# Six of 22 half-pairs of a feed-forward block's second product, by seven quarter products in place of eight

## The chip, the cores and the metric

The kernel runs on one core of a Trainium2 chip. The metric is the device time of one execution in microseconds (us). Five engines of the core work side by side, each through its own queue in order: PE (TensorE, the matrix products; PEld is its weight load), DVE (VectorE), ACT (ScalarE), POOL (GpSimd) and SP (SyncE, which issues the loads). They wait for each other by semaphores. SBUF holds the data in 128 partitions; products land in PSUM, eight banks of 128 x 512 float32 numbers.

## The reference, cut to what matters

One decoder layer on 512 tokens of width 1024, in float32. It is a sandwich: a feed-forward block, a token mixer (two kinds of recurrent heads), and a second feed-forward block, each with a norm ahead and one behind. The change concerns both feed-forward blocks.

```python
def swiglu_ffn(x, w_in, w_out):                       # w_in 1024 x 5632, w_out 2816 x 1024
    gate, up = jnp.split(x @ w_in, 2, axis=-1)
    return (jax.nn.silu(gate) * up) @ w_out           # "second product": 512 x 2816 by 2816 x 1024

x = x + 0.5 * rms_norm(swiglu_ffn(rms_norm(x, norm_pre[l, 0]), ffn1_w_in[l], ffn1_w_out[l]), norm_post[l, 0])
x = x +       rms_norm(token_mixer(rms_norm(x, norm_pre[l, 1]), ...), norm_post[l, 1])
x = x + 0.5 * rms_norm(swiglu_ffn(rms_norm(x, norm_pre[l, 2]), ffn2_w_in[l], ffn2_w_out[l]), norm_post[l, 2])
```

## The kernel before, in words

**Three matmuls for one product.** PE multiplies in the type float32r. To keep float32 accuracy each operand is split into a high part (a copy by ACT, which rounds) and a low part (a subtraction by DVE), and `mm3` (L125) issues three matmuls: high by high, high by low, low by high (L127, L128, L129). An operand so split is called a tile here; making one is a *cast*, one ACT copy and one DVE subtraction over 128 x 1024 numbers. A matmul keeps a 128 x 128 block (the stationary side, PEld) in the array and moves 256 or 512 columns through it.

**First product** (`ffn_in`, L654, and `prod`, L476). It already goes by a seven-product scheme (p1 to p7, in an order written down in `ORDER`), with matmuls of 256 columns at L489. Its results, after SiLU and the product with the up half, are kept in `hf` (22 x 512 numbers in each partition: the hidden activations, transposed).

**Second product** (`ffn_out`, L676). The 2816 hidden rows are cut in 11 *pairs* of 256 rows, and the 1024 outputs in two halves of 512 columns. A pair in one half is a *half-pair*: 256 rows by 512 tokens by 512 columns, 24 matmuls of 512 columns (four blocks of 128 tokens, two blocks of rows, three matmuls each, L690). The loop at L701 goes over the 11 pairs, half 0 first, into four PSUM banks `acc`, one for each block of 128 tokens. For each half-pair it needs one weight tile and one activation tile:

- `pull` (L243) gives the next weight tile; `feed` and `split` (L186 to L226) cast weights ahead, in the order of a list of items (`ffn_items`), until WBUF = 4 tiles are alive or ready. Their four slots lie next to each other in one tensor `w`; `drop` (L250) frees a slot when its matmuls are done.
- `h_tile` (L666, casts L672 and L673) makes the activation tile in a ring of three buffers, two or three ahead (`more`).

After the first half-pair, the last of the seven products of the first product (p4 of the last tile) is done in between (L489, 24 matmuls). When half 0 is done, `post0` (L377) takes its squares (ACT L354) and its product with the gain (DVE L383). In half 1 the last four half-pairs (LAST = 4) are done block by block by `last` (L406): for each block `i` of 128 tokens the 24 matmuls that are left (six for each of the four pairs), then `post1` (L386: squares, two small POOL instructions L355 and L359, DVE L391 and L395), then `after(i)`: in the first block the next norm (`pre`, L362, DVE L373), in the second the store of the output. `trans` turns the normed tokens for the mixer (PE L268, ACT L274, DVE L275), and `head4` / `head_mm` (L439 to L455) starts the mixer's first four weight columns, 24 matmuls of 256 columns each (L444). `last` and what follows are put in order by the framework's scheduler; the order on each engine is then fixed in the program.

**Alignment.** `place` (L232), PAD, LATE and the `late` choice in `split` shift tiles by 64 to 448 bytes against each other.

Of the kernel before, what the change touches and what calls it, by code (L numbers as in the profile page):

```python
# [20 lines left out]
NF = FF // P  # L21
EPS = 1e-6
RAW, WBUF, PAD, LATE, NEAR = 3, 4, 128, 112, 48
PAIRS = NF // 2
HALF = T // 2
# [25 lines left out]
class Load:  # L51


    def __init__(self, key, src, a, b, ring="raw", depth=3, ahead=3, group=None):
        self.key, self.src, self.a, self.b, self.ring, self.depth, self.ahead = key, src, a, b, ring, depth, ahead
        self.group = group


class Item:

    def __init__(self, key, loads, rows=None, adds=(), dst=None):
        self.key, self.loads, self.rows, self.adds, self.dst = key, loads, rows, adds, dst
        self.reads = {key, *(k for pair in adds for k in pair)}


class Layer:
    def __init__(self, ctx, tc, aps):
        self.tc, self.nc = tc, tc.nc  # L70
        self.__dict__.update(aps)
        nc = self.nc
        pool = lambda name, **kw: ctx.enter_context(tc.tile_pool(name=name, bufs=1, **kw))
        self.cp, self.wp, self.sp, self.psp = pool("cp"), pool("wp"), pool("sp"), pool("psp", space=PSUM)
        self.dp = pool("dp", space=bass.MemoryType.DRAM)
        self.uid, self.hold = 0, ()
# [18 lines left out]
    def col(self, n=1):  # L95
        return self.sp.tile([P, n], F32, tag=f"col{n}", bufs={1: 12}.get(n, 4), name=self.name("col"))
# [89 lines left out]
    def split(self):  # L186

        nc = self.nc
        it = self.items.popleft()
        raw = self.raw[it.key]  # L190
        _, a, b = raw.shape
        if it.dst:
            w = it.dst()
        else:
            if self.wt is None:
                self.wt = self.wp.tile([P, 2 * D * WBUF + PAD], F32R, name="w")
# [7 lines left out]
            self.slot[id(w)] = n, late, w  # L204
        hi, lo = self.both(w)
        self.ready.append((w, it.dst is not None))
        rows = it.rows
        if rows is None:
            nc.scalar.copy(hi, raw)  # L209
            yield  # L210
            nc.vector.tensor_tensor(lo, raw, hi.bitcast(F32), op=ALU.subtract)  # L211
        else:
            for j in range(a):
                nc.scalar.activation(hi[:, j], raw[:, j], AF.Copy, scale=rows[:, j : j + 1])
            yield
            for j in range(a):
                nc.vector.scalar_tensor_tensor(
                    lo[:, j], raw[:, j], rows[:, j : j + 1], hi[:, j].bitcast(F32), op0=ALU.mult, op1=ALU.subtract
                )
        with self.behind(*self.hold):  # L220
            for out, other in it.adds:
                o, c = self.raw[out], self.raw[other]
                nc.gpsimd.tensor_tensor(o, o, c, op=ALU.add)  # L223
        self.load_due(self.done)
        self.done += 1
        yield  # L226

    def both(self, w):

# [41 lines left out]
    def two(self, dst, i, src):  # L271

        v = slice((i % 2) * P, (i % 2 + 1) * P)
        self.nc.scalar.copy(dst[:, 0, :, v], src)  # L274
        self.nc.vector.tensor_tensor(dst[:, 1, :, v], src, dst[:, 0, :, v].bitcast(F32), op=ALU.subtract)  # L275
# [387 lines left out]
        self.feed()  # L663
        self.lag()

    def h_tile(self, k2, dst=None):  # L666

        t = dst
        if t is None:
            t = self.place(self.hpool.tile([P, 2 * D + PAD], F32R, tag="s", bufs=3, name=self.name("hs")), 2)  # L670
        src = self.hf[:, 2 * k2 : 2 * k2 + 2, :]
        self.nc.scalar.copy(t[:, 0], src)  # L672
        self.nc.vector.tensor_tensor(t[:, 1], src, t[:, 0].bitcast(F32), op=ALU.subtract)  # L673
        return t

    def ffn_out(self, gpost_row, scale, after, trans, head):  # L676
        NK2, LAST = PAIRS, 4
        seq = [k2 for _ in range(2) for k2 in range(NK2)]
        hs = self.hs
        made = [len(hs)]  # L680

        def more(n):
            while made[0] < min(n, len(seq)):
                k2 = seq[made[0]]
                last = made[0] == len(seq) - 1
                dst = self.xq[3].rearrange("p b k t -> p b (k t)").rearrange("p b (k t) -> p b k t", k=2) if last else None
                hs.append(self.h_tile(k2, dst))
                made[0] += 1

        def out_mm(ps, w, h, k2, i):  # L690
            for kk in range(2):
                k = 2 * k2 + kk
                s = slice(i * P, (i + 1) * P)
                self.mm3(ps, h[:, 0, kk, s], h[:, 1, kk, s], w[:, 0, kk, :], w[:, 1, kk, :], k == 0, k == NF - 1)

        g = self.gain("gpost", gpost_row)
        ys = []
        n = 0
        for half in range(2):
            acc = [self.ps() for _ in range(NT)]  # L700
            for k2 in range(NK2 - LAST if half else NK2):  # L701
                more(n + 2)
                w = self.pull()
                more(n + 3)
                h = hs.popleft()
                for i in range(NT):
                    out_mm(acc[i], w, h, k2, i)
                self.drop(w)
                n += 1
                if n == 1:  # L710
                    self.prod("p4", PAIRS - 1)
                    self.after("p4", PAIRS - 1)
                self.lag()
            if half == 0:
                ys = [self.post0(acc[i], g, scale) for i in range(NT)]
        ws = []
        for k2 in range(NK2 - LAST, NK2):
            ws.append((k2, self.pull()))
            more(n + 1)
            n += 1  # L720
# [84 lines left out]
    def ffn_items(self, name, w_in, w_out):  # L805

        made = []
        place = {"p1": "a", "p2": "c", "p3": "d", "p4": "a", "p5": "a", "p6": "a", "p7": "b"}
        place.update({"c1": "a", "c2": "c", "c3": "b", "c4": "d"})
        adds = {}  # L810
# [21 lines left out]
        for p, t in ORDER:  # L832
            if p[0] == "e":
                continue
            dst = (lambda n=stay[p]: self.stay[n]) if p in stay else None
            made.append(Item((name, t, place[p]), own.get((p, t), ()), None, adds.get((p, t), ()), dst))
        for h in range(2):
            for k2 in range(PAIRS):
                src = w_out[k2 * 2 * P : (k2 + 1) * 2 * P, h * 512 : (h + 1) * 512].rearrange("(k p) d -> p k d", p=P)
                key = (name, "out", h, k2)  # L840
                made.append(Item(key, [Load(key, src, 2, 512, "raw2", 5, 8)]))
                if h == k2 == 0:
                    made.append(Item((name, PAIRS - 1, "a"), ()))
        return made

    def small_params(self):

# [711 lines left out]
```

## Time and profile before

| what | value |
|---|---|
| median of 3 runs | 937.39 us (937.3 to 937.43) |
| the profiled execution | 936.74 us, of which its span is 935.0 us |
| granted TensorE clock in it | 0.998 of full |
| PE busy / DVE busy / ACT busy / POOL busy | 926.7 / 700.1 / 468.7 / 289.9 us |
| matmuls | 7021 |
| first block: second product | about 225 to 350 us |
| second block: second product | about 806 to 928 us |

How to read it: the span is the time from the first to the last instruction of the profiled execution; a few microseconds of the execution lie around it. A busy engine is one that has an instruction in flight; neighbouring matmuls overlap, so the number that counts for PE is the distance from one start to the next. Rows of the groups give line, engine, operation, what is written and read, count, busy time and the mean of one in ns, and then the idle time ahead of them with the engine that ended it. In the table by stages each engine has its busy time and, in brackets, how many of its instructions touch the stretch; then come the granted clock (PEclk), the DMA share and GB/s.

### The profile page before, as it was taken

To read this page: it belongs to the slowest core of one execution; us is meant where nothing else is said; L and a number is where in the kernel's file an instruction comes from. 1 tells how busy PE (TensorE), PEld (TensorE's weight loads), DVE (VectorE), ACT (ScalarE), POOL (GpSimd) and SP (SyncE) were. 2 spreads that over 40 slices of the span, in tenths; PEclk is the share of its full clock that TensorE was granted. 3 is DMA by queue.
4 is the path that set the end of the run, shared out by engine and by line. 5 is a ranking of instruction groups with operands and counts; after the bars stand their busy time and mean duration, and the time that the engine had idled before them with its cause. 6 is when DMAs were issued, how large, how long until landed. Compare 5 with 4: busy or idle time off the path is not lost.

```text
span 935.0 us, 16820 instructions
## 1 busy us (share of the span) xinstructions
PE 926.7 (99%) x7021; PEld 850.6 (91%) x7021; DVE 700.1 (75%) x785; ACT 468.7 (50%) x639; POOL 289.9 (31%) x225
## 2 busy tenths in 40 slices
PE   9999999999999999999999999999999999999997
PEld 7999999999888889998888888999999999988885
DVE  6798999998545466688766655887999999844543
ACT  7645445455334345987654254853444454534431
POOL 3535555661000027000020301445455655100001
PEclk9999999999999999999999999999999999999999
DMA  9243334425323005422423135213333422332202
GB/s 318 89 136 114 113 97 131 128 99 158 113 91 106 7 3 126 108 83 70 136 70 113 46 108 185 90 46 113 114 111 117 134 91 91 116 110 91 91 0 91
DMA packets 81992, 97.10 MB, mean 104 GB/s; under 512 B 4178, under 2 KB 61558, under 8 KB 81915
## 3 DMA queue, kind: packets, MB, share of 16 engines
q1 hardware_dynamic: 81306, 94.44, 32.4%
q8 instruction: 55, 0.90, 0.4%
q0 software_dynamic: 320, 1.06, 0.3%
q10 hardware_dynamic: 288, 0.52, 0.2%
q14 instruction: 23, 0.18, 0.1%
HBM read 93.90 MB, written 2.11 MB: 103 GB/s over the span
## 4 chain that ended last, share of the span: by engine, by line
PE 97%; DVE 1%; POOL 1%; issue 1%; ACT 1%; DVEq 0%; POOLq 0%; ACTq 0%
PE ps L489 46%; PE ps L127 13%; PE ps L129 13%; PE ps L128 13%; PE ps L434 6%; PE ps L268 1%; PE ps L1058 1%; POOL col L355 0%; PE ps L1328 0%; PE ps L1131 0%; PE ps L1296 0%; PE ps L116 0%; ACT junk L354 0%; PE ps L123 0%; PE ps L1097 0%
## 5 line engine op out<-in xcount | busy, mean ns | idle before, releaser
L211 DVE TENSOR_TENSOR w<-raw,w 128x1024 fp32r<-128x1024 f32 x214 | 364.2, 1710 | 129.5 <-ACT w L209 129.5
L209 ACT CAST w<-raw 128x1024 fp32r<-128x1024 f32 x214 | 223.9, 1052 | 305.6 <-PE ps L129 104.5
L223 POOL TENSOR_TENSOR raw<-raw,raw 128x1024 f32<-128x1024 f32 x80 | 221.0, 2763 | 171.8 <-DVE w L211 161.3
L489 PE MATMUL ps<-xq,w 128*128 128x256 f32 x2016 | 238.1, 277 | 0.0
L489 PEld LDWEIGHTS ps<-xq,w 128*128 128x128 f32 x2016 | 233.7, 188 | 0.2
L489 PE MATMUL ps<-sq,w 128*128 128x256 f32 x1440 | 171.0, 277 | 0.0
L489 PEld LDWEIGHTS ps<-sq,w 128*128 128x128 f32 x1440 | 167.4, 188 | 0.0
L129 PE MATMUL ps<-w,hs 128*128 128x512 f32 x336 | 131.0, 390 | 0.0
L127 PE MATMUL ps<-w,hs 128*128 128x512 f32 x336 | 130.9, 390 | 0.0
L128 PE MATMUL ps<-w,hs 128*128 128x512 f32 x336 | 130.8, 389 | 0.0
L127 PE MATMUL ps<-w,xq 128*128 128x512 f32 x208 | 83.2, 400 | 0.1
L128 PE MATMUL ps<-w,xq 128*128 128x512 f32 x208 | 81.0, 390 | 0.0
L129 PE MATMUL ps<-w,xq 128*128 128x512 f32 x208 | 81.0, 391 | 0.0
L129 PEld LDWEIGHTS ps<-w,hs 128*128 128x128 f32 x336 | 63.1, 188 | 13.8 <-DVE hs L673 0.7
L127 PEld LDWEIGHTS ps<-w,hs 128*128 128x128 f32 x336 | 63.1, 188 | 13.0
L128 PEld LDWEIGHTS ps<-w,hs 128*128 128x128 f32 x336 | 63.1, 188 | 12.8
L355 POOL TENSOR_SCALAR col<-col 128x1 f32<-128x1 f32 x24 | 10.5, 437 | 198.8 <-ACT junk L354 198.6
L434 PE MATMUL ps<-xq,w 128*128 128x256 f32 x480 | 55.8, 278 | 0.0
L434 PEld LDWEIGHTS ps<-xq,w 128*128 128x128 f32 x480 | 55.4, 188 | 0.2 <-issue 0.2
L673 DVE TENSOR_TENSOR hs<-hf,hs 128x1024 fp32r<-128x1024 f32 x42 | 51.1, 1217 | 0.0
L355 POOL TENSOR_SCALAR col<-col,col 128x1 f32<-128x1 f32 x24 | 10.0, 418 | 119.5 <-ACT junk L354 119.2
L129 PEld LDWEIGHTS ps<-w,xq 128*128 128x128 f32 x208 | 39.0, 188 | 8.8 <-DVE xq L275 0.3
(233 smaller groups left out, 939.5 us busy)
## 6 DMA issues: line engine op xcount, KB each, us to landing
raw<-in_ffn_w_in_dram SPq DMA_DIRECT2D x88, 512.0 KB, 4.4
raw<-in_ffn_w_out_dram SPq DMA_DIRECT2D x44, 512.0 KB, 3.9
raw<-in_w_mix_in_dram SPq DMA_DIRECT2D x28, 512.0 KB, 3.8
raw<-in_w_mix_out_dram SPq DMA_DIRECT2D x8, 512.0 KB, 3.7
out_dram<-xs SPq DMA_DIRECT2D x8, 256.0 KB, 2.1
xs<-in_x_dram SPq DMA_DIRECT2D x6, 256.0 KB, 6.2
gpost<-in_norm_post_dram SPq DMA_DIRECT2D x3, 512.0 KB
gpre<-in_norm_pre_dram SPq DMA_DIRECT2D x2, 512.0 KB, 4.1
```

The costliest lines, as they stand in the source:

```text
L127: mm(ps, sh, mh, start=start, stop=False, **kw)
L128: mm(ps, sh, ml, start=False, stop=False, **kw)
L129: mm(ps, sl, mh, start=False, stop=stop, **kw)
L209: nc.scalar.copy(hi, raw)
L211: nc.vector.tensor_tensor(lo, raw, hi.bitcast(F32), op=ALU.subtract)
L223: nc.gpsimd.tensor_tensor(o, o, c, op=ALU.add)
L268: self.nc.tensor.transpose(pt[:, c * P : (c + 1) * P], src[:, k * P : (k + 1) * P], self.ident)
L355: nc.gpsimd.tensor_scalar(m, ss, s2 / D, b, op0=ALU.mult, op1=ALU.add)
L434: mm(ps[:, u0:u1], w[:, a, k, :], self.xop(k, b, u0, u1), start=k + n + m == 0, stop=k == ND - 1 and n == 2, skip_group_check=True,)
L489: self.nc.tensor.matmul(ps[:, c], wb[b][:, k, v], left[d][:, k, :], start=first and a + n + k == 0, stop=n == 2 and k == KH - 1, skip_grou ...
L673: self.nc.vector.tensor_tensor(t[:, 1], src, t[:, 0].bitcast(F32), op=ALU.subtract)
L1058: nc.tensor.matmul(sc[r, o : o + u.stop - u.start], k8[:, m, r], q8[:, m, u], start=True, stop=True, skip_group_check=True)
```

## The change

An order for the half-pairs of each half is written down in `OUT`. The letter says how a pair is done: `p` plain as before; `r` plain, with the activation tile that half 0 left in its buffer; `k` and `s` by seven quarter products (*fast* pairs here). So three of 11 in each half are fast: pairs 3, 4 and 2.

A fast pair cuts its 256 rows by 512 tokens by 512 columns into quarters and does seven products of 256 tokens by 128 rows by 256 columns, each as two blocks of tokens by three matmuls of 256 columns: 42 matmuls in place of 24. It needs two weight tiles and two activation tiles: the plain ones and those of sums and differences of quarters. The weight sums are made by `w_sums` in place in the loaded weights (four DVE subtractions of 128 x 256) and cast as a second item into a second slot; the activation sums by `s_tile` (four DVE operations of 128 x 256) and one more cast. A `k` pair's two activation tiles stay in the four `xq` buffers for half 1; those of `s` are made in both halves. Casts marked `defer` are held back and issued behind the next cast.

Products 2, 3 and 4 add straight into `acc`; 1, 5, 6 and 7 add over the three pairs of a half into four more banks `sums`. After the last fast pair `gather` makes four terms of the sums (one ACT copy, four DVE additions of 128 x 512) in rows of `hf` that are free by then, and behind the next half-pair's matmuls four DVE additions put them into `acc`. All eight PSUM banks are in use. In half 1 four activation tiles fewer are made (`r` and `k`).

The loop and the four weight tiles of the end stand in `manual_schedule`: there the program's order is the order on the engines. In `last`, blocks 0 and 1 are now done together, and only then `post1` for both. The weight slots lie 2 D + 128 numbers apart, so 512 bytes more than before, and `late` is set by item: 64 bytes for plain second products and for the mixer's 512-wide weights, 128 for fast pairs.

```diff
+OUT = ("p0 p1 k3 p5 k4 p6 s2 p7 p8 p10 p9".split(), "r9 k3 r10 k4 p0 s2 p1 p5 p6 p7 p8".split())
...
-            taken = {(n, late) for n, late, _ in self.slot.values()}
-            fit = [(n, late) for late in (True, False) for n in self.free if (n - 1 if late else n + 1, not late) not in taken]
-            n, late = next(f for f in fit if not f[1] or (it.key[0] == "mix" and b == 512))
-            self.free.remove(n)
-            o = PAD + 2 * D * n - 16 * late
+            n = self.free.popleft()
+            o = PAD + (2 * D + 128) * n - 16 * (it.late if it.late is not None else b == 512)
...
+    def cast(self, hi, lo, src, defer=False):
+        nc = self.nc
+        late, self.pend = self.pend, ()
+        steps = [
+            lambda: nc.scalar.copy(hi, src),
+            lambda: nc.vector.tensor_tensor(lo, src, hi.bitcast(F32), op=ALU.subtract),
+        ]
+        if defer:
+            self.pend, steps = steps, ()
+        for n in range(2):
+            for f in (*steps[n : n + 1], *late[n : n + 1]):
+                f()
...
+        def seven(acc, sums, begun, w, wt, h, hs_, stop):
+            tok = lambda q, t: slice(HALF * q + P * t, HALF * q + P * (t + 1))
+            col = lambda q: slice(HALF * q, HALF * (q + 1))
+            for p, a, ka, qa, b, kb, qb in (
+                (1, h, 0, 0, w, 0, 0), (5, hs_, 1, 1, wt, 0, 0), (6, hs_, 0, 0, wt, 1, 1), (7, hs_, 0, 1, wt, 0, 1),
+                (2, h, 1, 0, w, 1, 0), (3, hs_, 1, 0, w, 1, 1), (4, h, 1, 1, wt, 1, 0),
+            ):
...
+                    for m, (x, y) in enumerate(((0, 0), (0, 1), (1, 0))):
+                        self.nc.tensor.matmul(
+                            out, a[:, x, ka, tok(qa, t)], b[:, y, kb, col(qb)],
...
+        def gather(sums, pairs):
...
+            self.flush()
+            self.nc.scalar.copy(x[:, :, 0], two(sums[1]))
+            add(two(u), two(sums[6]), x[:, :, 0])
+            add(x[:, :, 1], two(sums[5]), two(u))
+            add(y[:, :, 0], two(sums[7]), two(u))
+            add(y[:, :, 1], two(sums[5]), y[:, :, 0])
...
+                for m, k2, kind in todo:
+                    more(n + 2)
+                    w = self.pull()
+                    wt = self.pull() if kind in "ks" else None
+                    more(n + 3)
+                    h, hs_ = hs.popleft()
+                    if kind in "pr":
+                        for i in range(NT):
+                            out_mm(acc[i], w, h, i, m == 0, bool(terms) or m == PAIRS - 1)
+                        if terms:
+                            for i in range(NT):
+                                add(acc[i], acc[i], terms[i])
+                            terms = None
+                    else:
+                        seven(acc, sums, begun, w, wt, h, hs_, k2 == fast[-1])
+                        self.drop(wt)
+                    self.drop(w)
+                    if fast and k2 == fast[-1]:
+                        terms = gather(sums, [k for _, k, kind in self.outs(0) if kind == "k"])
...
         def mm(i):
-            for m, (k2, w) in enumerate(ws):
-                out_mm(acc[i], w, hs[m], k2, i)
+            for m, (k2, w) in enumerate(ws if i != 1 else ()):
+                for j in (0, 1) if i == 0 else (i,):
+                    out_mm(acc[j], w, hs[m][0], j, False, m == LAST - 1)
...
+    def w_sums(self, raw):
+        sub = lambda out, a, b: self.nc.vector.tensor_tensor(out, a, b, op=ALU.subtract)
+        (b11, b12), (b21, b22) = ((raw[:, k, :HALF], raw[:, k, HALF:]) for k in range(2))
+        sub(b11, b12, b11)
+        sub(b12, b22, b12)
+        sub(b22, b22, b11)
+        sub(b21, b21, b22)
+
+    def s_tile(self, k2, dst=None, whole=False):
...
+        tt(s1, a22, a21, ALU.add)
+        tt(s3, a11, a21, ALU.subtract)
+        tt(s2, s1, a11, ALU.subtract)
+        tt(s4, a12, s2, ALU.subtract)
+        if not whole:
+            return self.h_tile(k2, dst, True)
```

More of the change, by code (lines that the diff above doesn't have):

```diff
@@ L59, with __init__ @@
 class Item:
-    def __init__(self, key, loads, rows=None, adds=(), dst=None):
-        self.key, self.loads, self.rows, self.adds, self.dst = key, loads, rows, adds, dst
+    def __init__(self, key, loads, rows=None, adds=(), dst=None, then=None, late=None, defer=False):
+        self.key, self.loads, self.rows, self.adds, self.dst, self.then, self.late = key, loads, rows, adds, dst, then, late
+        self.defer = defer
         self.reads = {key, *(k for pair in adds for k in pair)}
@@ L208, in split @@
         if rows is None:
-            nc.scalar.copy(hi, raw)
-            yield
-            nc.vector.tensor_tensor(lo, raw, hi.bitcast(F32), op=ALU.subtract)
+            yield from self.cast(hi, lo, raw, it.defer)
         else:
@@ L223, in split @@
                 nc.gpsimd.tensor_tensor(o, o, c, op=ALU.add)
+        if it.then:
+            it.then(raw)
         self.load_due(self.done)
@@ new lines, in seven @@
+        def seven(acc, sums, begun, w, wt, h, hs_, stop):
[5 more added lines that the diff above has]
+            ):
+                fresh = p in sums and p not in begun
+                begun.add(p)
+                for t in range(2):
+                    if p in sums:
+                        out = sums[p][:, col(t)]
+                    else:
+                        out = acc[2 * (p == 4) + t][:, col(p == 3)]
+                    for m, (x, y) in enumerate(((0, 0), (0, 1), (1, 0))):
+                        self.nc.tensor.matmul(
+                            out, a[:, x, ka, tok(qa, t)], b[:, y, kb, col(qb)],
+                            start=fresh and t + m == 0, stop=stop and m == 2, skip_group_check=True,
+                        )
@@ L698, in ffn_out @@
         n = 0
[L699 to L708, printed above, removed]
-                n += 1
[L710 to L715, printed above, removed]
```

101 lines of the change are left out of this document (74 added, 27 removed).

## The prediction, made before the changed kernel had run

> **What bounds the kernel now.** I read the page's engine table and slices first, then the table by stages, then the chain.
>
> ```profile
> span 935.0 us, 16820 instructions
> PE 926.7 (99%) x7021; PEld 850.6 (91%) x7021; DVE 700.1 (75%) x785; ACT 468.7 (50%) x639; POOL 289.9 (31%) x225
> PE   9999999999999999999999999999999999999997
> PEclk9999999999999999999999999999999999999999
> ```
> ```profile
> 225.00:350.00 125.00, 125.00 (x573) 103.89 (x573) 64.59 (x67) 52.21 (x73) 8.02 (x19) 1.00 0.22 72
> 350.00:364.00 14.00, 13.80 (x118) 13.25 (x117) 11.50 (x16) 6.27 (x13) 8.96 (x22) 1.00 0.61 153
> 806.00:928.00 122.00, 122.00 (x550) 101.21 (x549) 58.42 (x57) 43.84 (x55) 3.83 (x10) 1.00 0.25 82
> ```
>
> PE has work in flight in every slice, at the full granted clock. The second products are the first and the third row of the stages: PE 125.0 of 125.0 and 122.0 of 122.0 us, VectorE only 64.6 and 58.4. So in these stages every start-to-start distance on PE is on the path, and VectorE, ScalarE and the DMAs (share 0.22 and 0.25) have room *on average*. A gain must come from fewer or shorter matmuls; a loss from any moment at which PE waits for VectorE. Both occur here.
>
> What a matmul costs is the distance between starts, not its "mean ns":
>
> ```profile
> 20.47 0.87 PE ps L268 x8
> ...
> 47.86 177.59 PE ps L489 x1560
> ...
> 230.91 2.83 PE ps L489 x24
> ...
> 811.35 2.83 PE ps L489 x24
> ```
> ```profile
> 240.00:340.00 100.00, 100.00 (x442) 82.51 (x441) 47.17 (x45) 38.70 (x50) 4.34 (x11) 1.00 0.19 64
> ```
> ```profile
> 341.28 0.39 PE L127 MATMUL ps<-w,xq 128*128 128x512 f32 x1
> ...
> 342.43 0.39 PE L129 MATMUL ps<-w,xq 128*128 128x512 f32 x1
> ```
>
> The chain gives 256-column matmuls 177.59/1560 = 114 ns in the long first product, but 2.83/24 = 118 ns where the same product stands between 512-column ones (both blocks). The 512-column ones: 442 instructions touch 100 us of pure second product, so 100/441 = 227 ns; the two timeline rows, five starts apart, give 1.15/5 = 230 within their rounding. I take 227.
>
> VectorE and ScalarE in the same stage:
>
> ```profile
> L211 DVE TENSOR_TENSOR w<-raw,w 128x1024 fp32r<-128x1024 f32 x17 | 20.8, 1225 | 47.0 <-ACT w L209 47.0
> L673 DVE TENSOR_TENSOR hs<-hf,hs 128x1024 fp32r<-128x1024 f32 x17 | 20.7, 1218 | 0.0
> L209 ACT CAST w<-raw 128x1024 fp32r<-128x1024 f32 x17 | 17.9, 1053 | 52.3 <-PE ps L129 42.0 <-issue 10.3
> ...
> L354 ACT ACTIVATE junk<-ps 128x512 f32<-128x512 f32 x4 | 2.4, 596 | 1.5 <-PE ps L129 1.5
> ```
> ```profile
> L508 DVE TENSOR_TENSOR q<-ps,u 128x512 f32<-128x512 f32 x20 | 13.7, 683 | 5.2 <-PE ps L489 5.1
> L1350 DVE TENSOR_TENSOR y<-ps,col 128x256 f32<-128x256 f32 x8 | 3.0, 420 | 6.6 <-POOL col L1347 6.6
> ```
> ```profile
> 283.82 1.22 DVE L211 TENSOR_TENSOR w<-raw,w 128x1024 fp32r<-128x1024 f32 x1 [3.08 <-ACT w L209]
> 284.96 1.22 DVE L673 TENSOR_TENSOR hs<-hf,hs 128x1024 fp32r<-128x1024 f32 x1
> 286.10 1.28 DVE L383 TENSOR_TENSOR y<-ps,gpost 128x512 f32<-128x512 f32 x2
> ```
>
> A low part takes 1.22 us, a 512-wide operation 0.68, a 256-wide one 0.42 (nearest row, with a PSUM source). But a queue that is full moves on faster: the starts at 283.82, 284.96 and 286.10 are 1.14 apart, so 0.08 of each instruction overlaps the next. In a full queue I count 1.14, 0.60 and 0.34 us; the high part on ScalarE 1.05.
>
> **The change, part by part.** Sums are for both blocks and against the profiled execution (936.74 us).
>
> *1. Matmuls.* Six fast half-pairs a block, twelve in all. Removed: 12 x 24 = 288 of 512 columns, 288 x 0.227 = 65.4 us. Added: 12 x 42 = 504 of 256 columns. At 118 ns that is 59.5 us, a gain of **5.9 us**; at 114 it is 57.5, a gain of 7.9. I take 118, since its two rows stand where the fast pairs will stand, between 512-column matmuls. So even with no stall the change can bring 0.8% at most.
>
> [...]
>
> *2. More casts and sums on VectorE.* A fast pair adds a second weight cast, a second activation cast and eight 256-wide operations: 2 x 1.14 + 8 x 0.34 = 5.0 us. In half 0 a fast and a plain pair together ask VectorE for six low parts and eight small ones, 9.6 us, against PE's 42 x 0.118 + 24 x 0.227 = 10.4. It fits, by 0.8. The tightest place is pair k4. After p4's product (a 24-matmul island that VectorE must wait for) its queue holds in order: two 0.60 ones, low parts of p5's weights, k3's second weights, p5's activations, k4's weights, four sums, k4's activations, four sums, k4's second activations, p6's weights, k4's second weights: 1.2 + 8 x 1.14 + 8 x 0.34 = 13.0 us, plus an estimated 3 us of hand-overs with ScalarE (three high parts of 1.05 that VectorE cannot cover, among them the one that starts only behind the sums). PE needs the last one after p1, k3, p5 and the first quarter product: 5.45 + 4.96 + 5.45 + 0.7 = 16.6. So k4 is met by a few tenths or missed by a few; s2 has the same recurrence. I take nothing, with 0.3 us for each of six such waits (k4 and s2 in half 0, s2 in half 1, in both blocks; 1.8 in all) at the upper end and 1.3 each if the instructions do not overlap. What hides this work is only that margin.
>
> *3. A new wait: the four terms.* Here the change pays. After the last fast pair (s2) the changed program's order on VectorE is: low part of the next-but-one activations, four gather additions, low parts of two weight tiles, low part of one more activation tile, and only then the four additions into `acc`. The plain pair behind s2 runs meanwhile, 24 x 0.227 = 5.45 us. The pair after it adds into `acc[0]` and must wait for the first of the four additions. From the end of s2 the first low part starts at 0.6 (its high part, 1.05, can start about 0.45 before that end, when the sixth quarter product has freed its buffer). Then 1.14 + 4 x 0.60 + 3 x 1.14 + 0.68 = 7.6. Together 8.2 against 5.45: PE stands still for **2.8 us**. Later blocks of `acc` need 0.60 each against PE's 1.36, so they do not wait again. The order is the same in half 1 (activations, gather, two weights, activations, additions), so four times in all: **+11.2 us**. Bounds: 2.0 each if the first high part finds its buffer sooner, 3.7 without the overlap of instructions (4 x 1.22 + 5 x 0.68 + 0.9 = 9.2). PE is the bound afterwards too, so nothing gives it back. Queued behind the four additions are only a weight and an activation tile that PE needs some 9 us later.
>
> *4. Blocks 0 and 1 together at the end of a block.* The end of the first block overlaps norm and transposes with the last products:
>
> ```profile
> 342.94 0.70 ACT junk L354 x2
> ...
> 343.73 0.81 POOL col L355
> ...
> 344.61 0.56 POOL col L359
> ...
> 345.19 0.76 DVE xs L395
> ```
> ```profile
> 349.92 3.25 PE L444 MATMUL ps<-xq,w 128*128 128x256 f32 x24
> 353.00 1.03 PE L268 MATMUL ps<-ident,xn 128*128 128x128 f32 x8
> 353.79 5.70 PE L444 MATMUL ps<-xq,w 128*128 128x256 f32 x48
> 359.66 1.29 PE L268 MATMUL ps<-ident,hf 128*128 128x128 f32 x8 [0.17 <-DVE hf L373]
> 360.71 2.98 PE L444 MATMUL ps<-xq,w 128*128 128x256 f32 x24
> 363.53 0.73 PE L434 MATMUL ps<-xq,w 128*128 128x256 f32 x5
> ```
>
> From 342.94, behind a block's last product, to the end of the last row and of a second addition like it (0.7) pass 3.7 us: the new `xs`. Before, block 0 began this 5.45 us ahead of block 1; now both begin at block 1's time, and two chains of norms follow each other on ScalarE, POOL and VectorE. In the changed order the low part of the mixer's first weight tile stands on VectorE behind block 3's `xs`: last product + one ScalarE cast in the way (1.05) + 3.7 + 1.14 = 5.9 us. PE has until then 8 + 16 matmuls of 114 ns and 8 transposes, about 3.7: a wait of 2.2. The second weight tile's low part comes behind the norm of block 3 (0.4 to 0.7 more), and the transposes of blocks 1 and 2 come a few tenths late each, 0.9 in all: 3.6. The head stage lasts 363.53 - 349.92 = 13.6 us now, of which 96 x 0.114 + 16 x 0.109 (transposes, 0.87/8) = 12.7 is work: about 0.9 of waits goes. Net **+2.7 us**, between +1 and +5. The second block ends in stores; its last chain is block 3's alone, as before: 0.
>
> *5. The rest.* The bytes loaded are the same; in SP's order three of the mixer's loads come later, behind loads of the second product, but tens of microseconds ahead of their use. In half 1 the four banks of `sums` are those of half 0's `acc`: `post0` frees them (a square of 0.60 and a product of 0.64 us a bank) during r9's 5.45 us. Half 1 makes four activation tiles fewer, off the path. Slots 512 bytes apart keep all addresses equal within 512 bytes: 0, with 0.3 either way.
>
> Sum: 936.74 - 5.9 + 11.2 + 2.7 = 944.7. The median of the runs is 0.65 above the profiled execution: **945.4 us**.
>
> **The rivals.**
>
> *A, faster: the terms are hidden.* One mechanism, at the pair behind s2: if the first addition into `acc` ends within 5.45 us of s2's end, term 3 is 0. It needs the queue ahead of it to be 2.8 us shorter, for instance if VectorE did the three low parts behind the additions. Then 937.39 - 5.9 + 2.7 = 934.2, or 932.2 at 114 ns. For it: VectorE is busy for half of this stage on average. Against it: the order is fixed in the program, and all nine durations are rows of this stage. With only part hidden (1 us left each) it is 938.2, no difference.
>
> *B, slower still: VectorE becomes the bound.* If queued instructions do not overlap here (the new 256-wide ones depend on each other), six waits of 1.3 at k4 and s2 and 3.7 at each of the terms: 945.4 + 7.8 + 3.6 = 956.8. For it: a margin of 0.8 in 10.4 us. Against it: the pitch of 1.14 in the timeline.
>
> [...]
>
> **How the numbers follow.** Forecast 945.4: 0.69. Within it, 114 ns takes 2.0, the bounds of the terms are -3.2 and +3.6, of the end -1.7 and +2.3, of the small waits +1.8. Not all ends come together; two of them move it to 940 or 951. A hidden: 0.11; A in part: 0.08; B: 0.10; C: 0.02. A measurement of this kernel can tell about 0.2%, 1.9 us, from no change. Range 938.5 to 951: it leaves out A hidden, C and most of B, about 2 in 10. Faster 0.11, same 0.09, slower 0.80.
>
> **What would show it.** Right: PE idle for 2 to 4 us at the second plain pair behind s2, four times, ended by VectorE's addition into `ps`; 504 matmuls at 114 to 118 ns; the head stage near 16 us. Wrong: no such idle (A), idle at the second quarter product of k4 and s2 (B), or fast matmuls above 125 ns (C).

## The result, and the profile after

The changed kernel takes **961.33 us** (median of 5 runs, 959.42 to 961.87) against 937.3 (5 runs, 936.7 to 937.43): a ratio of 1.0254, 95% interval 1.0239 to 1.0269. The forecast was 945.4, in a range from 938.5 to 951. The sign was right; the loss is 24 us where 8 were forecast. The profiled execution is one of 961.87 us, 25.1 above that of the kernel before.

The page of the changed kernel, engine table and slices, against the same rows of before (PE 99%, every slice 9):

```profile
span 960.2 us, 17399 instructions
PE 932.7 (97%) x7237; PEld 863.1 (90%) x7237; DVE 765.2 (80%) x911; ACT 482.1 (50%) x657; POOL 288.3 (30%) x225
PE   9999999999989898999999999999999999998987
PEclk9999999999989999999999999999999999999999
```

PE is no longer always in work: slices 12, 14, 16, 37 and 39 (24 us each) have holes, all of them in the two second products and the head behind the first; the last slice had one before. Slice 12 of the granted clock is below 9 too, which the prediction did not expect at all. The table by stages shows both (columns as in the prediction):

```profile
225.00:350.00 125.00, 117.55 (x633) 101.52 (x632) 88.62 (x114) 50.61 (x63) 1.70 (x7) 0.96 0.28 85
350.00:364.00 14.00, 12.06 (x65) 9.80 (x64) 9.60 (x15) 10.07 (x23) 5.89 (x14) 1.00 0.00 0
268.00:272.00 4.00, 4.00 (x19) 3.14 (x17) 3.93 (x6) 2.46 (x3) 0.00 (x0) 1.00 0.12 47
275.50:281.00 5.50, 5.50 (x14) 4.25 (x14) 3.61 (x5) 0.00 (x0) 0.00 (x0) 0.50 0.54 177
```

In the second product PE is busy for 117.55 of 125 us, where it was 125 of 125. The third and fourth rows lie on the two sides of one wait. From 268 to 272 the clock is 1.00; from 275.5 to 281 it is **0.50**, and PE, busy throughout, has only 14 matmuls in 5.5 us. What PE waits for (total, times, longest):

```profile
PE ps L129 <- DVE ps L755: 6.0, 2, 3.0
PE ps L129 <- ACT xq L232: 6.0, 2, 3.0
PE ps L738 <- DVE w L233: 3.1, 6, 0.7
PE ps L464 <- DVE w L233: 1.8, 2, 1.0
...
PE ps L288 <- DVE hf L393: 1.2, 1, 1.2
PE ps L288 <- DVE xn L393: 0.7, 1, 0.7
```

The first two rows are the four waits for the terms. In half 1 the table names an ACT cast, which ended at 335.09, 0.15 behind VectorE's first addition (334.26 + 0.68) and 0.01 ahead of PE's start. In half 0 PE starts 0.15 behind the addition too, and in e2 below, with one cast less ahead of the addition, all four waits carry its name (DVE ps L755); so I take the ACT row for a coincidence. The third row is the second weights of k4 and s2, the rest is the head. PE and VectorE at the first wait, from the timeline:

```profile
271.80 0.39 PE L131 MATMUL ps<-w,hs 128*128 128x512 f32 x1
275.20 0.77 PE L129 MATMUL ps<-w,hs 128*128 128x512 f32 x1 [3.01 <-DVE ps L755]
275.77 0.63 PE L130 MATMUL ps<-w,hs 128*128 128x512 f32 x1
276.19 0.63 PE L131 MATMUL ps<-w,hs 128*128 128x512 f32 x1
...
280.89 0.54 PE L130 MATMUL ps<-w,hs 128*128 128x512 f32 x1
281.27 0.39 PE L131 MATMUL ps<-w,hs 128*128 128x512 f32 x1
```
```profile
267.17 1.23 DVE L233 TENSOR_TENSOR hs<-hf,hs 128x1024 fp32r<-128x1024 f32 x1 [2.14 <-ACT hs L232]
268.32 0.68 DVE L755 TENSOR_TENSOR u<-ps,hf 128x512 f32<-128x512 f32 x1
269.03 1.29 DVE L755 TENSOR_TENSOR hf<-ps,u 128x512 f32<-128x512 f32 x2
270.35 0.69 DVE L755 TENSOR_TENSOR hf<-ps,hf 128x512 f32<-128x512 f32 x1
270.96 2.35 DVE L233 TENSOR_TENSOR w<-raw,w 128x1024 fp32r<-128x1024 f32 x2
273.23 1.22 DVE L233 TENSOR_TENSOR hs<-hf,hs 128x1024 fp32r<-128x1024 f32 x1
274.37 1.88 DVE L755 TENSOR_TENSOR ps<-ps,hf 128x512 f32<-128x512 f32 x3
```

From 271.80 to 275.20 are 3.40 us, less the normal 0.227 a wait of 3.17. Then come starts 427 ns apart (275.77, 276.19 and on) until 281.27, where 227 returns. The VectorE queue is the one that the prediction wrote down: a low part, four gather additions, three low parts, then the addition that PE waits for.

Where the 25.1 us are (start-to-start distances of the trace, both blocks):

| term | forecast | measured | how |
|---|---|---|---|
| fast matmuls | -5.9 | -6.0 | an undisturbed fast pair takes 4.95 (42 x 117.8 ns), a plain one 5.45; 12 pairs |
| second weights of k4 and s2 | 0 | +4.2 | six pairs take 5.86, 5.23, 5.86, 5.72, 5.37, 5.86, less 6 x 4.95 |
| wait for the terms | +11.2 | +12.6 | 3.17 + 3.14 + 3.17 + 3.14 |
| slow matmuls behind it | none | +7.8 | what 7 to 14 starts lost against 227 ns: 2.89 + 1.65 + 1.67 + 1.54 |
| head of the mixer | +2.7 | +4.7 | first transposes to the long product: 20.9 before, 25.6 after |
| long product behind the head | 0 | +1.4 | 306 matmuls, see below |
| start-up | 0 | +0.6 | the second product starts at 225.9, before at 225.3 |

The last but one row is also a row of the chain, before and after:

```profile
363.69 34.68 PE ps L434 x306
```
```profile
378.87 36.04 PE ps L454 x306
```

### The profile page after: what moved, and what is told of

Its sections match the earlier page's. It is cut to its first block, busy times and chain, and to the rows that moved or that the text cites. A ratio compares the mean times of both kernels' runs of the same rounds, so it can differ in the third digit from the quotient of the medians.

```text
span 960.2 us, 17399 instructions
## 1 busy us (share of the span) xinstructions
PE 932.7 (97%) x7237; PEld 863.1 (90%) x7237; DVE 765.2 (80%) x911; ACT 482.1 (50%) x657; POOL 288.3 (30%) x225
## 4 chain that ended last, share of the span: by engine, by line
PE 55%; DVE 4%; ACT 2%; issue 1%; POOL 0%; DVEq 0%; POOLq 0%; ACTq 0%
PE ps L509 22%; PE ps L129 7%; PE ps L131 7%; PE ps L130 7%; PE ps L454 6%; PE ps L738 1%; DVE w L233 1%; PE ps L1170 1%; PE ps L464 1%; PE ps L288 1%; ACT hs L232 1%; DVE hs L233 1%; DVE raw L933 1%; ACT w L232 1%; ACT junk L374 0%
## 5 line engine op out<-in xcount | busy, mean ns | idle before, releaser
L233 DVE TENSOR_TENSOR w<-raw,w 128x1024 fp32r<-128x1024 f32 x226 | 372.6, 1661 | 63.7 <-ACT w L232 63.6
L232 ACT CAST w<-raw 128x1024 fp32r<-128x1024 f32 x226 | 235.0, 1051 | 247.0 <-POOL raw L220 88.2
L129 PE MATMUL ps<-w,hs 128*128 128x512 f32 x240 | 97.4, 406 | 12.0 <-DVE ps L755 6.0
L130 PE MATMUL ps<-w,hs 128*128 128x512 f32 x240 | 96.3, 401 | 0.0
L131 PE MATMUL ps<-w,hs 128*128 128x512 f32 x240 | 96.1, 400 | 0.0
L375 POOL TENSOR_SCALAR col<-col 128x1 f32<-128x1 f32 x24 | 7.2, 299 | 208.1 <-ACT junk L374 208.0
L129 PEld LDWEIGHTS ps<-w,hs 128*128 128x128 f32 x240 | 46.8, 195 | 22.8 <-ACT hs L232 13.6
L131 PEld LDWEIGHTS ps<-w,hs 128*128 128x128 f32 x240 | 46.8, 195 | 10.3
L130 PEld LDWEIGHTS ps<-w,hs 128*128 128x128 f32 x240 | 47.1, 196 | 9.2
L233 DVE TENSOR_TENSOR hs<-hf,hs 128x1024 fp32r<-128x1024 f32 x32 | 39.0, 1218 | 12.2 <-ACT hs L232 12.1
```

Source lines behind the costliest of these rows:

```text
L129: mm(ps, sh, mh, start=start, stop=False, **kw)
L130: mm(ps, sh, ml, start=False, stop=False, **kw)
L131: mm(ps, sl, mh, start=False, stop=stop, **kw)
L232: lambda: nc.scalar.copy(hi, src),
L233: lambda: nc.vector.tensor_tensor(lo, src, hi.bitcast(F32), op=ALU.subtract),
L375: nc.gpsimd.tensor_scalar(m, ss, s2 / D, b, op0=ALU.mult, op1=ALU.add)
```

## The experiments

The theory behind the first runs: the order on VectorE makes the wait for the terms, and this wait makes the slow matmuls. The rival: the slow clock belongs to the mixture of long and short matmuls.

**e1_terms_first.**

```diff
-                    more(n + 2)
-                    w = self.pull()
+                    if not terms:
+                        more(n + 2)
+                    w = self.pull(feed=not terms)
                     wt = self.pull() if kind in "ks" else None
-                    more(n + 3)
+                    if not terms:
+                        more(n + 3)
```

> The changed kernel, but on VectorE the four additions into acc come directly behind the gather additions; the casts of two weight tiles and one activation tile that stood between them follow. Theory: the wait for the terms is made by those three low parts, and the slow matmuls behind it (10 to 14 of 512 columns at 427 ns in place of 227) are made by the wait. In the changed kernel's trace the first gather addition starts at 268.32, the last ends at 271.0; the first addition into acc would then end at 271.7, ahead of the next pair's start at 272.0, so the wait should be 0 and so should the slow matmuls: 4 x 3.15 = 12.6 us and 7.9 us less, 961.3 - 20.5 = 941 (939 to 943). Rival 1: the slow clock belongs to the fast pairs themselves: then only the waits go, 949. Rival 2: the additions also delay the casts, which PE then waits for at the next pair but one: part of the 12.6 comes back, 945 or more.

942.57 us (4 runs, 941.96 to 942.88), 18.8 less than the changed kernel. Every plain stretch behind an s2 runs through: 120 matmuls in 27.21 us, 227 ns each, at full clock. So the order was the cause of all four waits, and without the waits there are no slow matmuls behind s2; rival 1, at 949, is out. Of the 20.5 us expected 1.7 are missing, and they are in the head, whose waits (transposes, L288) have grown. Behind the longest of them the clock is at half from 352.07 to 355.49, the one such stretch in this trace:

```profile
PE ps L738 <- DVE w L233: 3.2, 6, 0.7
PE ps L288 <- DVE xn L393: 2.7, 2, 1.4
PE ps L288 <- DVE hf L393: 2.0, 1, 2.0
```

**e2_one_cast_behind.**

```diff
-                    more(n + 3)
+                    if not terms:
+                        more(n + 3)
```

> The changed kernel, but of the three low parts ahead of the additions into acc only the activation tile's goes behind them; the two weight tiles' stay ahead. It shortens the wait by 1.14 us a time, from 3.15 to 2.0. Theory: the slow matmuls come only when PE stands still for longer than some limit between 2.0 and 3.15 us; so no slow matmuls here, and the time is 961.3 - 4 x 1.14 - 7.9 = 949 (947 to 951). Rival 1: any wait of this kind is followed by slow matmuls: 961.3 - 4.6 = 957. Rival 2: the slow matmuls come in proportion to the wait: about 954.

951.1 us (4 runs, 949.69 to 952.23). The four waits came out at 2.05 us each. Behind three of them the matmuls keep 227 ns; behind the fourth, of the same length, eight run slow (1.63 us lost):

```profile
859.90 0.39 PE L131 MATMUL ps<-w,hs 128*128 128x512 f32 x1
862.17 0.47 PE L129 MATMUL ps<-w,hs 128*128 128x512 f32 x1 [1.88 <-DVE ps L755]
...
862.71 0.39 PE L131 MATMUL ps<-w,hs 128*128 128x512 f32 x1
```
```profile
915.76 0.39 PE L131 MATMUL ps<-w,hs 128*128 128x512 f32 x1
918.04 0.47 PE L129 MATMUL ps<-w,hs 128*128 128x512 f32 x1 [1.88 <-DVE ps L755]
...
918.96 0.63 PE L129 MATMUL ps<-w,hs 128*128 128x512 f32 x1
919.38 0.63 PE L130 MATMUL ps<-w,hs 128*128 128x512 f32 x1
```

For the profiled execution (950.05) the sum closes: 961.87 - 4.45 (waits) - 7.8 + 1.6 - 1.4 (the long product, back at 34.68 us) = 949.8. Both rivals are out for a wait of 2 us, but the theory, which had no slow matmuls at 2 us, failed at the fourth wait: the length alone does not decide.

**e3_idle_alone** and **e9_short_idle** ask whether a wait alone does it, with nothing of the change. Both add zeros, so nothing of the computation is left out.

```diff
+CHAIN = (
+    {(0, 2): C(8), (0, 4): C(9), (0, 6): C(9, 1), (0, 8): C(10), (1, 1): C(10, 1), (1, 3): C(11), (1, 5): C(13)},
+    {(0, 2): C(12), (0, 4): C(11), (0, 6): C(10, 1), (0, 8): C(10), (1, 1): C(9, 1), (1, 3): C(9), (1, 5): C(16)},
+)
...
                 for i in range(NT):
                     out_mm(acc[i], w, h, k2, i, i == 0 and (half, k2) in CHAIN[self.block])
+                for v in CHAIN[self.block].get((half, k2), ()):
+                    self.nc.vector.tensor_tensor(acc[0][:, :v], acc[0][:, :v], zero[:, :v], op=ALU.add)
```

(C(n, m) is n additions 512 wide and m 256 wide; the loop stands in `manual_schedule`. e9 has chains of 4 to 7.)

> The kernel before, with nothing of the change, but behind seven plain pairs of each block's second product VectorE adds zeros to the first block of acc 8 to 16 times in a chain, so that PE waits at the next pair: by 0.66 us an addition, estimated waits of 1.6 to 6.8 us. Theory: slow matmuls (427 ns) follow a wait from about 3 us on and none shorter than about 2.5; the slow stretch lasts 2 to 6 us whatever the length of the wait. Rival: no wait here is followed by slow matmuls, since it is the mixture with 256-column products that makes them. The time itself is of no interest (about 940 plus the waits, some 50 us, and the slow matmuls).

> As e3_idle_alone (the kernel before with chains of zero additions on VectorE into the first block of acc), but 4 to 7 additions in a chain. In e3_idle_alone an addition of the chain cost 0.73 us and 8 of them made PE wait 4.1 us, so here 1.2, 1.6, 2.0, 2.4, 2.7, 3.1 and 3.4 us, each twice. There every wait (4.1 to 10 us) was followed by 6 to 14 slow matmuls (1.4 to 2.9 us lost) whatever its length; the one-cast kernel had four waits of 2.05 us, one of them with slow matmuls behind it; the changed kernel waits of 3.15 us with slow matmuls behind all four. Theory: below 1.8 us never, from 3.1 us always, between them sometimes, and the loss is again 1.4 to 2.9 us whatever the wait. Rival: the loss grows with the wait, so that the short ones lose well under 1.4 us.

The times are 1051.34 us (e3) and 977.91 us (e9), one run each. In e3 the waits came out longer than meant, 4.1 to 10 us, and all fourteen were followed by 6 to 14 slow matmuls, a loss of 1.4 to 2.9 us. In e9, in order of length: 1.16, 1.21, 1.63, 1.67, 1.90, 1.90, 2.37, 2.37 us: no slow matmul; 2.63: once none, once seven; 3.10: none; 3.14, 3.37, 3.41: 8, 7 and 7. Two of them from the timeline of e9:

```profile
320.50 0.39 PE L134 MATMUL ps<-w,hs 128*128 128x512 f32 x1
323.82 0.47 PE L132 MATMUL ps<-w,hs 128*128 128x512 f32 x1 [2.94 <-DVE ps L718]
324.13 0.39 PE L133 MATMUL ps<-w,hs 128*128 128x512 f32 x1
```
```profile
875.88 0.39 PE L134 MATMUL ps<-w,hs 128*128 128x512 f32 x1
878.73 0.77 PE L132 MATMUL ps<-w,hs 128*128 128x512 f32 x1 [2.47 <-DVE ps L718]
879.30 0.63 PE L133 MATMUL ps<-w,hs 128*128 128x512 f32 x1
```

The longer wait goes by without a trace, the shorter is followed by seven slow matmuls. So a wait alone does it, with no mixture of products, and the loss does not grow with the wait: where there is one it is 1.4 to 1.7 (6 to 8 slow starts, about 3 us at 427 ns) or 2.2 to 2.9 us (10 to 14). Below 2.0 us no wait did it, from 3.14 on all did, between them some; the theory's "from 3.1 us always" missed the 3.10.

The traces show what lies between, for they keep the moments at which the granted clock changes. In the twelve traces of this case it goes 28 times to half (14 in e3, four each in the changed kernel, e6 and e9, one each in e1 and e2) and 28 times back while PE has work, and each of the 56 changes lies a whole number of 3.413 us behind the trace's first change (0.003 us off at most): in the changed kernel 2, 18, 19, 175, 176, 192 and 193 times behind the one at 274.38. The stretches of this grid are called windows here; they do not begin with a wait. The two waits above, each with the window that holds most of it and the next one:

```profile
321.99:325.40 3.41, 1.58 (x7) 1.35 (x8) 3.34 (x5) 0.92 (x1) 0.00 (x0) 1.00 0.00 0
325.40:328.81 3.41, 3.41 (x17) 2.80 (x16) 0.54 (x1) 0.00 (x0) 0.00 (x0) 1.00 0.00 0
874.95:878.36 3.41, 1.31 (x6) 0.75 (x4) 3.27 (x5) 1.99 (x2) 0.00 (x0) 1.00 0.36 132
878.36:881.77 3.41, 3.04 (x7) 2.48 (x8) 2.49 (x3) 0.00 (x0) 0.00 (x0) 0.50 0.22 60
```

The longer wait is cut by the end of a window: 1.10 us of its idle time lie in one, 1.83 in the next. The shorter has 2.10 in one window, and the next one runs at half. In all twelve traces each of the 28 windows ahead of a change to half had PE idle for at least 1.88 us (1.88 at e2's fourth wait, 2.19 to 2.88 in the changed kernel), and no other window at full clock had more than 1.84. Behind a window at half clock the full one came back where PE was idle in it for at most 0.54 us (0.37 in the last row), and not where for 0.74 or more (0.82 in the changed kernel from 274.38 to 277.79); the slow matmuls filled one window or two, and a window full of them cost 1.6 us (3.41 less 227/427 of it). By these figures (an estimate) a wait with about 3.0 us idle, as the four of the changed kernel, meets a half-clock window about four times in five, depending on where it falls; that all four did is in part chance.

Twelve waits from 2.05 to 3.37 us in the second products of these runs, each shorter than one window, were followed by slow matmuls, the four of the changed kernel and the four of e6 among them.

**e4_slots_alone** and **e5_slots_and_tiles.** The first has the weight slots of the change (512 bytes apart, 64 bytes shift), the second also its activation tiles:

```diff
-            t = self.place(self.hpool.tile([P, 2 * D + PAD], F32R, tag="s", bufs=3, name=self.name("hs")), 2)
+            t = self.place(self.hpool.tile([P, 2 * D + PAD], F32R, tag="s", bufs=3, name=self.name("hs")), 2, True)
```

> The kernel before with one part of the change alone: weight slots 512 bytes apart, and the shift of 64 bytes for every 512-wide weight tile. The prediction costs this part at 0. Theory 1: no difference (936.5 to 938). Theory 2: the first product behind the first block's end, whose 306 matmuls take 117.8 ns in the changed kernel and 113.3 before, takes 117.8 here too, because the addresses set it: 938.7. If those matmuls stay at 113.3, the addresses have nothing to do with it.

> The kernel before with the whole of the change's placement: weight slots 512 bytes apart, the shift of 64 bytes for 512-wide weights, and the activation tiles of the second product 448 bytes further on, which e4_slots_alone left out. In e4_slots_alone the 512-wide matmuls of the second products came out at 233.3 ns in place of 227.3. Theory: it is the distance between the weight tile and the activation tile that sets this, and with both moved it is 227.3 again and the time that of the kernel before, 937 to 938.5. Rival: the spacing of 512 bytes itself costs 6 ns a matmul, and the changed kernel's 227 comes from something else: 943.

e4: 943.43 us (4 runs), 1.0061 of before (1.0046 to 1.0076). The loss is not where theory 2 has it: the 306 matmuls stay at 113.3 ns, but every plain matmul of the second product costs 233.3 ns in place of 226.7. In the table by stages, e4 and then e5 for the same 100 us:

```profile
240.00:340.00 100.00, 100.00 (x430) 80.45 (x429) 44.86 (x42) 38.57 (x48) 2.39 (x7) 1.00 0.20 64
```
```profile
240.00:340.00 100.00, 100.00 (x442) 82.57 (x441) 46.61 (x44) 39.25 (x50) 4.28 (x11) 1.00 0.19 64
```

430 matmuls touch it in e4, 442 in e5 and (as the prediction shows) before. e5: 936.99 us (10 runs), 0.9995 (0.9986 to 1.0005). So the whole placement of the change is worth 0, but only as a whole.

**e6_last_apart.**

```diff
-            for m, (k2, w) in enumerate(ws if i != 1 else ()):
-                for j in (0, 1) if i == 0 else (i,):
-                    out_mm(acc[j], w, hs[m][0], j, False, m == LAST - 1)
+            for m, (k2, w) in enumerate(ws):
+                out_mm(acc[i], w, hs[m][0], i, False, m == LAST - 1)
```

> The changed kernel with the last four pairs done block by block again, as before the change (blocks 0 and 1 no longer together). The trace of the changed kernel has 25.6 us from the first transposes at the end of the first block to the mixer's first long product, before 20.9: 4.7 more, where the prediction had 2.7. Theory: all of it comes from blocks 0 and 1 starting their norms together; undone, the time is 961.3 - 4.7 = 956.6 (955.5 to 958). Rival: part of the wait is owed to VectorE, which still has the terms' additions and the casts held up by them in its queue when the norms come; then less than 2.5 comes back, 959 or more.

954.31 us (4 runs, 952.97 to 955.26), 7.0 less (6.6 between the profiled executions), more than the theory. First transposes to the long product: 21.4 us where the changed kernel has 25.6, so 4.2 for the head; 1.4 more because the 306 matmuls behind it are back at 34.68 us; and 1.3 because the slow matmuls of the profiled execution lost 6.5 us and not 7.8: all four waits cost one window at half clock, where the first of the changed kernel cost two. The rival (under 2.5) is out.

**e7_second_weights_first** (on top of e1).

```diff
-                    made.append(Item(key, (), late=2, defer=True))
+                    made.append(Item(key, (), late=2))
```

> As e1_terms_first, and in addition the cast of a fast pair's second weight tile is no longer held back behind the next pair's weight cast but issued ahead of it. In e1_terms_first PE waits 0.93 us at the second quarter product of k4 and of s2 in half 1 and 0.58 at s2 in half 0, each for VectorE's low part of the second weights, which stands 1.14 us behind another low part that is not needed yet. With the sevenths' own slower rhythm these six waits are 4.2 us by the pairs' sums (5.72 + 5.38 + 5.88 and 5.75 + 5.37 + 5.72 against 6 x 4.95). Theory: moved ahead by 1.14, all six vanish: 942.6 - 4.2 = 938.4 (937.5 to 939.5). Rival: the dependent chains of four 256-wide operations (0.45 us each) set the pace, and the wait moves to the next tile in the queue: 941 or more.

937.74 us (10 runs), 4.8 less than e1. All twelve fast pairs now take 4.95 us, and no row of L738 is left among the waits:

```profile
PE ps L288 <- DVE xn L393: 3.5, 2, 2.3
PE ps L288 <- DVE hf L393: 2.0, 1, 2.0
```

One low part out of the way, 1.14 us, was enough for all six. This makes the kernel as fast as the one before (1.0005, 0.9996 to 1.0014); the 5.9 us saved on matmuls are still lost, in the head.

**e8_three_edits.** e7 and e6 together.

> All three edits together: the terms' additions ahead of the casts, the second weights ahead of the next weights, and the last four pairs block by block as before. In e1_terms_first the stretch from the last s2's end to the mixer's long product is 49.4 us, of which about 42.6 would be there with the head of the kernel before; so 6.8 should go beside the 4.2 of the second weights: 942.6 - 4.2 - 6.8 = 931.6 (930 to 934), which is the kernel before less the 5.9 us that the matmuls save. Rival: block 0's norm still waits for VectorE, and 2 to 4 us stay: 934 to 936.

936.13 us (11 runs, 935.61 to 936.74), 0.9988 of before (0.9979 to 0.9996): of the 6.8 us for the head only 1.6 came back, and the rival was right. My reading, which no run tests by itself, is that without the wait for the terms VectorE has no pause either in which to catch up. The waits stand at the head although blocks 0 and 1 are apart:

```profile
PE ps L464 <- DVE w L233: 1.9, 2, 1.1
PE ps L288 <- DVE hf L393: 1.6, 1, 1.6
```

The order in the program differs too: the head's matmuls (L464) come in pieces of 8 and 16 between the transposes, as in the changed kernel, while in e6 and before they come in columns of 24.

**e10_terms_earlier** (on top of e8).

```diff
-"r9 k3 r10 k4 p0 s2 p1 p5 p6 p7 p8"
+"r9 k3 k4 r10 s2 p0 p1 p5 p6 p7 p8"
```

> As e8_three_edits, with the fast pairs of the second half one pair earlier (r9 k3 k4 r10 s2 p0 p1 in place of r9 k3 r10 k4 p0 s2 p1), so that two plain pairs in place of one lie between the last fast pair and the last four. In e8_three_edits the stretch from the last s2 of the first block to the mixer's long product takes 47.7 us, of which 42.6 is work; before the change the waits at that place came to 0.9. Theory: those waits come from the casts which the terms' additions push back into the time of the norms, and from the order that results on PE; one pair earlier they go, and the time is 936.1 - 4.2 = 932 (931 to 933.5), so that all of the 5.9 us saved on matmuls shows. Rival: k3 and k4 side by side need four weight tiles in a row from VectorE, and PE waits for one to two microseconds there in each block: 934 to 936.

**931.91 us** (5 runs, 931.36 to 932.63), 0.9938 of before (0.9925 to 0.9952): faster than both kernels, and where it was expected. PE is busy again in the whole second product, VectorE for four fifths of it:

```profile
225.00:340.00 115.00, 115.00 (x645) 100.86 (x645) 92.20 (x119) 53.51 (x69) 3.98 (x12) 1.00 0.31 92
```

Its fast matmuls keep the 117.8 ns, so the saving on matmuls that the prediction worked out (5.9) is what is measured (937.56 - 931.91 = 5.65) once no wait eats it. k3 and k4 side by side cost nothing (84 matmuls in 9.89 us). At the head one wait of 0.7 is left, and its matmuls come in columns of 24 again. So the casts' room and the order on PE changed together, and which of the two made the gain no run separates.

## Why the prediction was right in its sign and wrong in its size

The profiled execution lies 17.1 us above the 944.7 of the sum. The step that failed most is in term 3: it prices the wait for the terms by its length alone and puts nothing for what comes behind it. The runs showed 7.8 us of matmuls at half the clock there (point 3). Next comes "I take nothing" for the waits at k4 and s2, with 4.2 us (point 2); the rest are 2.0 us at the head, 1.4 in the length of the wait, 1.4 in the long product and 0.6 at the start.

1. *Matmuls: right.* 118 ns was taken; 117.8 was measured in the six undisturbed pairs, and behind their waits the other six ran on at 117.8 (three) or at 113 to 114 (three). e10 shows the gain in full. C, fast matmuls above 125 ns, is out.
2. *More casts and sums on VectorE: wrong.* The step that failed here is "I take nothing" for k4 and s2, with 0.3 each at the upper end; they cost 0.7 each on average. The list of what stands in the queue was right, its pace was not: I counted 0.34 for a 256-wide operation, as the 0.42 of a row less an overlap of 0.08 that was seen between instructions that do not depend on each other. The sums do:

```profile
245.19 1.80 DVE L942 TENSOR_TENSOR hf<-hf 128x256 f32<-128x256 f32 x4
248.10 1.23 DVE L233 TENSOR_TENSOR xq<-hf,xq 128x1024 fp32r<-128x1024 f32 x1 [1.12 <-ACT xq L232]
249.25 2.35 DVE L233 TENSOR_TENSOR w<-raw,w 128x1024 fp32r<-128x1024 f32 x2
```

   Four take 1.80, 0.45 each; eight in the queue ahead of k4 make about 0.9 more than counted, against a margin of 0.6. p4's product ends at 234.16 and VectorE at 251.6, 17.4 us where 16.6 were to be had; the other 0.5 are hand-overs with ScalarE, which I had as an estimate. This is rival B's mechanism at these pairs, to which I gave 0.10; e7 shows that one low part less ahead of the second weights takes all six waits away.
3. *The terms: the mechanism was right, the size was not.* The queue, its first start (0.60 behind s2's end in both) and the place are as the prediction has them. The wait is 3.15 and not 2.8, since the gather additions also depend on each other (2.64 in place of 2.40) and PE starts 0.15 behind VectorE's end. That is 1.4 us in all. The larger error, 7.8 us, is in the step that prices the wait by its length alone: four times 2.8. Behind the four waits of the changed kernel (3.14 to 3.17 us) the clock was at half for 3.41 us (three) or 6.83 (the first); in e9 the waits of 3.14, 3.37 and 3.41 us were followed by 7 or 8 slow matmuls, the one of 3.10 by none. The trace of before has no wait of PE above 0.2 us behind the first matmul, so it could not show this.
4. *Blocks 0 and 1 together: mis-sized.* +2.7 taken with a bound of 5; 4.7 measured, of which e6 gives back 4.2. The transposes (L288) wait 1.2 and 0.7 us where the prediction has 0.9 in all. The 1.4 us of the long product are not in the prediction.
5. *The rest at 0: right in sum, for an incomplete reason.* "Slots 512 bytes apart keep all addresses equal within 512 bytes" names only the weights; e4 shows that without the activation tiles' 448 bytes it would have been +5.8.

Rival A was priced at 934.2. e1 does just what it asks for, the addition ahead of the three low parts, and gives 942.6: 4.1 of the difference are the second weights (5.72 + 5.38 + 5.88 + 5.75 + 5.37 + 5.72 less 6 x 4.95), the rest is in the head and in the long product behind it. Only with the order of e10 does the gain come through.

## What to carry to other kernels

Price a new wait of the bound engine not by its length alone: in these runs two microseconds of idle PE cost mostly two (three of e2's four waits of 2.05), three cost up to six (3.17 and 2.89 behind it), since a window of 3.413 us with 1.88 or more of idle PE in it was followed by one at half the clock. Keep a wait of PE short: none below 2.05 us was followed by slow matmuls here. Where an in-order queue makes the wait, look first for what stands ahead in it and is not needed yet; and follow the work that is pushed back to the next tight place, or the gain is lost there (e8), until something earlier gives it room (e10). For a chain take the distance of a chain: for the 256-wide sums here 0.45 us, not the 0.34 worked out from independent instructions.

## What was not expected of the hardware

- With the activation tiles 448 bytes further on and nothing else changed, a matmul of 512 columns took 226.7 ns in place of 233.3 (e5 against e4; 442 and 430 of them touch the same 100 us). What in the addresses does it is not shown.
- The 306 matmuls of 256 columns behind the head take 34.68 us (113.3 ns each) before and in e2, e6, e8 and e10, but 36.04 (117.8) in the changed kernel, e1 and e7. What chooses is open; in e1 the fast pair's matmuls behind five of the six waits run at 113 to 114, in undisturbed pairs at 117.8.
- The additions of e9's chain, 512 wide, each reading from PSUM what the one before it wrote there, start 0.73 us apart (six in 4.36); the four independent ones into acc in the changed kernel 0.60 (four in 2.48).
- All 56 changes of the granted clock while PE has work lie on a grid of 3.413 us, and each change to half came behind a window with at least 1.88 us of idle PE (55% of it). The slow stretches had two lengths, 6 to 8 or 10 to 14 matmuls, for one or two windows, whatever the wait ahead of them (4.1 to 10 us in e3).
